# Encoder layer on one core: buffers of the channel mixer as single places in a written order, a chunk's sums moved between products, operands at equal offsets modulo 512 bytes

## The chip, the cores and the metric

One core of a Trainium2 chip runs the whole kernel in one launch. The time is what the device takes for one execution, in microseconds (us). Five engines work side by side, each on its own list of instructions: TensorE (PE; its weight loads are listed as PEld), VectorE (DVE), ScalarE (ACT), GpSimd (POOL) and SyncE (SP). All transfers are issued by SP, one after the other, in the order in which the program writes them.

## The reference, cut to what matters

An encoder layer over 2048 tokens of width 1024: a norm, one input projection, two attention mixers, an output projection with a residual, then the channel mixer.

```python
h = rmsnorm(x, mlp_norm_g[l])
u = jnp.einsum('bsd,df->bsf', h, w_up[l])        # 1024 -> 4096
u = jnp.square(jax.nn.relu(u))
x = x + jnp.einsum('bsf,fd->bsd', u, w_down[l])  # 4096 -> 1024
```

The kernel computes each of the mixer's two products by a scheme with seven block products in place of eight (Strassen's, in Winograd's form): blocks of the left and right operand are first added and subtracted, and the seven results are added up to the four result blocks.

## The kernel before

**Stages.** Input projection (0 to 475 us of the profiled span), attention (to 1812), output projection (1830 to 2044), up projection (2044 to 2696), down projection (to 3352). Every operand of TensorE is split into two parts, high and low (`split`, L151: ScalarE makes a rounded copy, VectorE the remainder), and three matmuls (high by high, high by low, low by high) stand for one.

**Buffers.** `pool(name, n)` reserves n equal buffers; pools on the left side lie one behind the other in the order in which they are made, those on the right side are counted from the other end. A later pool lies over memory that an earlier, closed one left, and the first use of a buffer waits for the last use of what lay there. A tile taken from a pool with several buffers gets one that a planner picks.

**Output projection** (L590). Eight chunks `tc_` of 256 tokens, two blocks of 128 each. `prepare` (L651) loads and splits a chunk's left operand, even chunks into `om_a`, odd ones into `om_b`. `block` (L680) makes 48 matmuls (L691), adds the residual (L695), norms the block on ScalarE (`h_f`, L703, L705), transposes it on TensorE (L171) and stores it as blocks of the right operand (`hb_d`, L716). In the blocks where `th` is 1 (the second 512 tokens of each chunk of 1024, `c` being 0 or 1) it then loads the block's partner (`h_old`) and lets GpSimd make the four sums T1 to T4 (`right_sums`, L757), each stored to `ht_d`. Three products of the up projection are written into the last block (`mlp_first`, L861).

**Up projection** (L865). From here the order of all work is as written. The right operand (tokens) comes in two chunks `c` of 1024 tokens, the left one (weights) in 16 pairs of column groups. There are 16 rounds, rounds 0 to 7 for the first chunk, 8 to 15 for the second; a round has 14 products (r = 0 to 13), of two groups in turn, with 12 matmuls each (L846). In products 0 to 5 the moving operand is one of B11, B21, T2, which lie in `self.first` (pool `uf`, left side); in 6 to 13 it is T3, T1, B22 or T4 in `self.big` (`uh`, right side). The weights' split pieces lie in `uw` and `uw2` (right side). `after(s)` (L907) takes a product's result out of its bank: products i = 0, 2 and 3 of a group are copied by ScalarE (`uy`, L915) and a later product adds to the same bank, which starts it only when the copy is done; 1, 4 and 5 are added on VectorE (L888), all are squared on ScalarE (`act`, L892, L893), and GpSimd makes the sums of the down projection's operand (`us`, L904), stored to `us_d` a few products later. GpSimd also makes the sums of the weights (`up_sums`, L801, at r = 0, 5 and 8). All values of `after` lie in the 15 buffers of `uv`.

**Down projection** (L1059). 56 steps m: seven right blocks i by eight token blocks b, 48 matmuls each (L1147). A step's part of the program: the residual's load (`x1`), the operand's load two steps ahead (`u_load`, into `uf`), in the first 16 steps three loads and two GpSimd operations for a piece of the weights' block T2 (`t2`, L1114; its store is issued after the step's matmuls, and SP waits there for GpSimd), then the loads of the next block's weight pieces (`prepare_piece`, L1004, into `dra` and `drb`), the splits, the matmuls.

Of the kernel before, what the change touches and what calls it, by code (L numbers as in the profile page):

```python
# [46 lines left out]


class Builder:
    def __init__(self, nc, tc, ap):  # L50
        self.nc, self.tc, self.ap = nc, tc, ap

        self.raw, self.ops, self.W, self.PS, self.B, self.U, self.D, self.pending = ({} for _ in range(8))
        self.slots = 0

# [297 lines left out]
    def attention(self):  # L353


        with ExitStack() as es:
# [233 lines left out]
    def out_proj(self):  # L590
# [3 lines left out]
        with ExitStack() as es:  # L594
            pool = self.pools(es)

            m2b, xp, hp, hsp, stage = pool("om_b", 1), pool("ox", 2), pool("oh", 1), pool("ohs", 3), pool("ows", 1)
            wp = [pool(f"ow{j}", 1) for j in range(ND)]
            small = pool("osx", 2)
            psy, pst = pool("psy", 2, space=PSUM), pool("psto", 3, space=PSUM)  # L600

            early = ExitStack()
            pool = self.pools(early)
            mp, sm, m2a = pool("om", 6), pool("osm", 2), pool("om_a", 1)
            pss, psr = pool("psss", 1, space=PSUM), pool("psr", 2, space=PSUM)
# [74 lines left out]
            def block(tc_, b, before=None):  # L680
# [91 lines left out]
    def operand(self, c, n, both=True):  # L772

        if n in self.RIGHT[:3]:
            t = self.first.tile([P, 2, 4, 512], F32R, name=f"hop_{n}", tag="big")
        else:
            t = self.big.tile([P, 2, 4, 512], F32R, name=f"hop_{n}", tag="big")
        src = (self.hb_d if n[0] == "B" else self.ht_d)[c, self.PLACE[n]]
# [16 lines left out]
    def up_load(self, n):  # L795
        if n < 2 * self.NF:
            self.raw[n] = self.raws.tile([P, ND, 256], F32, name="wu_raw", tag="raw")
            f = n % self.NF
            self.dma(self.raw[n], self.ap["w_up"][0, :, f * 256 : f * 256 + 256].rearrange("(j p) f -> p j f", p=P))

    def up_sums(self, n, part):  # L801
# [6 lines left out]
        )  # L808
        x, y = (self.sums.tile([P, 4, P], F32, name="w_sum", tag="sum") for _ in range(2))
        if part == 0:  # L810
# [24 lines left out]
    def up_product(self, s):  # L835
# [3 lines left out]
        if start:  # L839
            pool = self.acc[0] if (n % 2, kind) in ((0, "Y"), (0, "X"), (1, "Y")) else self.acc[1]  # L840
            self.PS[n, kind] = pool.tile([P, 512], F32, name="ps" + kind, tag="acc")
        ps = self.PS[n, kind]
# [8 lines left out]
    def mlp_begin(self, early):  # L851

        early.close()
        self.wop = [self.right("uw", 7)]
        self.acc = [self.right("psua", 3, space=PSUM)]
        for s in range(7):
# [8 lines left out]
    def mlp_up(self, es):  # L865
# [17 lines left out]
        def v(name):  # L883
            return vp.tile([P, H], F32, name=name, tag="v")

# [10 lines left out]
        def store(s, n, name, t):  # L896

            c, f = divmod(n, self.NF)
            dst = self.us_d[self.LEFT.index(name), c * 4 : c * 4 + 4, :, f, :].rearrange("b p t -> p b t")
            later(s, lambda: self.dma(dst, t.rearrange("p (b t) -> p b t", t=P)))  # L900

# [5 lines left out]
        def after(s):  # L907
# [8 lines left out]
            elif i == 1:  # L916
                t = add("c11", ps, x.pop(0))
                x["a11"] = act(t, t)
                store(s + 2, n, "A11", t)
            elif i == 4:  # L920
                t = add("c22", ps, x.pop(3))
                x["z"] = add("z", ps, x.pop(2))
                x["a22"] = act(t, t)
                store(s + 2, n, "A22", t)
            elif i == 5:
                a21 = add("c12", ps, x.pop("z"))
                act(a21, a21)
                s1 = sub(a21, x["a22"], ALU.add)
                s3 = sub(x["a11"], a21)
                x["s2"] = sub(s1, x["a11"])  # L930
                for name, t in (("S1", s1), ("S3", s3), ("S2", x["s2"])):
                    store(s + 4, n, name, t)
            else:
                a12 = act(v("c21"), ps)
                store(s + 2, n, "A12", a12)
                store(s + 5, n, "S4", sub(a12, x["s2"]))
                del val[n]

        for s in self.EARLY:
# [9 lines left out]
        for s in range(last + 1):  # L949
# [54 lines left out]
    def prepare_piece(self, i, k):  # L1004

        terms = self.TERMS[self.ORDER[i]]
        a = self.da.tile([P, 512], F32, name="wd_a")
        self.dma(a, self.w_down(terms[0], k)[:, 0])
        if len(terms) > 1:
            b = self.db.tile([P, 512], F32, name="wd_b")  # L1010
            self.dma(b, self.w_down(terms[1], k)[:, 0])
# [3 lines left out]
    def prepare_early(self, k):  # L1015

        t = self.raws.tile([P, 4, 512], F32, name="wd_raw", tag="raw")
        self.dma(t, self.w_down(self.TERMS[self.ORDER[0]][0], k, 4))
# [3 lines left out]
    def fill_piece(self, i, k):  # L1022
        if not self.quad(i, k):
            self.D[i, k] = self.small_slot()
        elif k % 4 == 0:
            t = self.big.tile([P, 2, 4, 512], F32R, name="wd_q", tag="big")
            for q in range(4):
# [6 lines left out]
    def u_load(self, m):  # L1034
        if m < len(self.STEPS):
            i, b = self.STEPS[m]
            t = self.first.tile([P, 2, 4, 512], F32R, name="u_op", tag="big")
            self.U[m] = t.rearrange("p h a (k t) -> p h (a k) t", t=P)
# [20 lines left out]
    def mlp_down(self):  # L1059
# [4 lines left out]
        with ExitStack() as es:  # L1064
            pool = self.pools(es)
            self.da, self.db, keep, xp = pool("dra", 7), pool("drb", 2), pool("dk", 1), pool("dx", 4)
            psd = pool("psd", 4, space=PSUM)
# [15 lines left out]
            def x1(i, b):  # L1083
# [3 lines left out]
                half, dh = goes[n]  # L1087
                t = xp.tile([P, H], F32, name="x1")
                self.dma(t, self.x1_d[rows(half, b), dh * H : dh * H + H])
# [24 lines left out]
            def t2(k):  # L1114

                a, b, c = self.da.tile([P, H], F32, name="wd_a"), *(self.db.tile([P, H], F32, name="wd_b") for _ in range(2))
                self.dma(a, self.w_down("12", k)[:, 0])
# [7 lines left out]
            for m, (i, b) in enumerate(self.STEPS):  # L1125
                x = x1(i, b)
                if m:
                    self.u_load(m + 2)
                if m < 16:
                    behind.append(t2(m))  # L1130
                if i < 6:

                    for k in (6, 7) if b == 6 else (b,) if b < 6 else ():
                        self.prepare_piece(i + 1, k)
                    for k in {5: (8, 9, 10), 6: (11, 12), 7: (13, 14, 15)}.get(b, ()):
                        self.prepare_piece(i + 1, k)
                if m:
                    self.u_split(m + 1)
# [17 lines left out]
    def build(self):  # L1156
        tc = self.tc
        with tc.tile_pool(name="const", bufs=1) as const, tc.tile_pool(name="dram", bufs=1, space=DRAM) as dram:
# [4 lines left out]
            with ExitStack() as keep, ExitStack() as es:  # L1163

                self.first = self.pools(keep)("uf", 3)
                self.right = self.pools(keep, side="right")
                pool = self.pools(es)
                self.raws, self.sums = pool("uraw", 2), pool("usum", 6)
                self.out_proj()
# [47 lines left out]
```

## Time and profile before

| | |
|---|---|
| median of 3 runs | 3363.14 us (3354.39 to 3369.92) |
| the profiled execution | 3357.71 us, its span 3355.9 |
| TensorE busy | 3238.4 us, 96% |
| VectorE, GpSimd, ScalarE busy | 61%, 51%, 47% |
| transfers | 431.38 MB, mean 129 GB/s |

The span is what the profiler saw of the program, from the first instruction to the last. The rest of the time lies around it. Busy shares are means over stages with different limits; a stage is read from its own rows. A matmul's length in a row is longer than the distance to the next one, since matmuls overlap: the pace is read from start to start.

### The profile page before, as it was taken

The page shows a single profiled execution, that of the slowest core. Times are in us where ns is not written, and L with a number is a line of the kernel's source. Part 1 is how long each engine was busy: PE and PEld are TensorE (multiplying, and loading weights), DVE is VectorE, ACT ScalarE, POOL GpSimd, SP SyncE. Part 2 cuts the span into 40 slices and gives each one's busy share as a digit, 9 for nine tenths or more (in the row PEclk, how much of TensorE's full clock was granted, in tenths as well). Part 3 has the DMA queues.
Part 4 walks back from the last instruction along what each step waited for, and adds up shares of the span by engine and source line. Part 5 has one row for each costly group of instructions (what it writes and reads, how often), then busy time and mean ns, then how long its engine had stood idle before and what let it go on. Part 6 is the DMA issues. An engine that isn't in the chain of part 4 may idle for free. (4 is left out here: it accounts for less than half of the span.)

```text
span 3355.9 us, 43068 instructions
## 1 busy us (share of the span) xinstructions
PE 3238.4 (96%) x15584; PEld 2459.6 (73%) x15584; DVE 2043.7 (61%) x3672; ACT 1576.0 (47%) x2352; POOL 1716.8 (51%) x934
## 2 busy tenths in 40 slices
PE   7999989999999999999999998999899999899999
PEld 6888866666666666666656886888788877688887
DVE  6455547877878777777773554555755554444442
ACT  4222226666666666666664333555555532222221
POOL 3344426666676666766666123666566543314231
PEclk9999999999999999999998998999999999999999
DMA  6336291112112211211013676544645556645573
GB/s 197 109 100 212 88 240 32 29 45 81 43 32 62 73 35 29 77 46 29 29 32 121 213 238 210 151 144 138 226 144 164 180 200 236 237 168 186 202 247 116
DMA packets 402452, 431.38 MB, mean 129 GB/s; under 512 B 26912, under 2 KB 336288, under 8 KB 390336
## 3 DMA queue, kind: packets, MB, share of 16 engines
q1 hardware_dynamic: 402240, 428.64, 41.0%
q8 instruction: 122, 2.00, 0.2%
q14 instruction: 90, 0.74, 0.1%
HBM read 286.93 MB, written 150.01 MB: 130 GB/s over the span
## 5 line engine op out<-in xcount | busy, mean ns | idle before, releaser
L550 POOL TENSOR_TENSOR acc<-acc,pta 128x1024 f32<-128x1024 f32 x224 | 536.7, 2396 | 250.4 <-ACT pta L548 245.4
L1147 PE MATMUL pd<-wd_q,u_op 128*128 128x512 f32 x1728 | 416.1, 399 | 10.0 <-ACT wd_q L153 5.6
L426 DVE CUSTOM_DVE_ANT_0 Sm<-ps_s,T 128x512 f32<-128x512 f32 x512 | 338.2, 685 | 124.0 <-PE ps_s L421 121.8
L1147 PEld LDWEIGHTS pd<-wd_q,u_op 128*128 128x128 f32 x1728 | 328.4, 191 | 91.9 <-ACT wd_q L153 6.5
L548 ACT ACTIVATE pta<-ps_a 128x512 f32<-128x512 f32 x512 | 291.5, 594 | 206.4 <-PE ps_a L547 193.3
L446 POOL TENSOR_TENSOR Sm<-Sm 128x2048 f32<-128x2048 f32 x64 | 293.4, 4584 | 139.4 <-ACT Sm L445 139.4
L514 DVE TENSOR_REDUCE mxa<-ps_m 128x1 f32<-128x512 f32 x512 | 330.3, 683 | 55.8 <-PE ps_m L511 54.6
L421 PE MATMUL ps_s<-Kb,Qb 128*128 128x512 f32 x1024 | 305.7, 408 | 2.7 <-DVE mx L426 2.5
L437 ACT ACTIVATE Sm<-Sm,negm 128x2048 f32<-128x2048 f32 x128 | 256.6, 2005 | 88.2 <-DVE negm L435 80.5
L846 PE MATMUL psY<-hop_T,w_op 128*128 128x512 f32 x1152 | 281.0, 398 | 17.2 <-ACT uy L915 12.1
L557 PE MATMUL po_a<-pta,v_a 128*64 128x512 f32 x1024 | 280.4, 622 | 4.6 <-ACT pta L548 4.4
L846 PEld LDWEIGHTS psY<-hop_T,w_op 128*128 128x128 f32 x1152 | 219.6, 191 | 68.8 <-ACT uy L915 14.2
L546 PEld LDWEIGHTS ps_a<-Qa,Ka 128*128 128x128 f32 x512 | 96.3, 189 | 228.8 <-issue 196.6
L153 ACT CAST u_op<-u_op 128x2048 fp32r<-128x2048 f32 x56 | 106.7, 1907 | 309.4 <-DMA u_op<-us_d 309.4
L546 PE MATMUL ps_a<-Qa,Ka 128*128 128x512 f32 x512 | 233.2, 456 | 17.3 <-DVE vt L154 12.6
L1147 PE MATMUL pd<-w_op,u_op 128*128 128x512 f32 x960 | 234.9, 399 | 7.9 <-ACT w_op L153 4.8
L154 DVE TENSOR_TENSOR w_op<-w_sum,w_op 128x512 fp32r<-128x512 f32 x128 | 151.8, 1197 | 137.8 <-ACT w_op L153 137.7
L154 DVE TENSOR_TENSOR tl<-ptb,th 128x512 fp32r<-128x512 f32 x256 | 175.4, 685 | 79.3 <-ACT th L153 79.1
L1147 PEld LDWEIGHTS pd<-w_op,u_op 128*128 128x128 f32 x960 | 182.2, 190 | 53.5 <-ACT w_op L153 6.0
L475 PE MATMUL po_b<-th,Vb 128*128 128x256 f32 x1024 | 209.4, 288 | 9.3 <-ACT th L153 9.0
L421 PEld LDWEIGHTS ps_s<-Kb,Qb 128*128 128x128 f32 x1024 | 179.5, 191 | 47.0 <-DVE mx L426 11.0
L511 PE MATMUL ps_m<-Ka,Qa 128*128 128x512 f32 x512 | 201.2, 433 | 7.0 <-DVE mx L426 2.3
(229 smaller groups left out, 6905.3 us busy)
## 6 DMA issues: line engine op xcount, KB each, us to landing
u_op<-us_d SPq DMA_DIRECT2D x56, 1024.0 KB, 4.9
wu_raw<-in_w_up SPq DMA_DIRECT2D x32, 1024.0 KB, 6.1
us_d<-us SPq DMA_DIRECT2D x128, 256.0 KB, 3.1
us_d<-c SPq DMA_DIRECT2D x96, 256.0 KB, 6.1
wd_a<-in_w_down SPq DMA_DIRECT2D x96, 256.0 KB, 5.9
Qb<-qkT_d SPq DMA_DIRECT2D x128, 128.0 KB, 3.0
wd_b<-in_w_down SPq DMA_DIRECT2D x64, 256.0 KB, 5.5
Qa<-qkT_d SPq DMA_DIRECT2D x48, 256.0 KB, 4.8
```

The lines of the kernel that those rows point to most:

```text
L154: self.nc.vector.tensor_tensor(lo, src, as32(hi), ALU.subtract)
L421: nc.tensor.matmul(ps, Q[:, c, i, qb * P : (qb + 1) * P], K[c][:, ks], start=(i == 0), stop=(i == 1))
L426: nc.vector.tensor_tensor_reduce(out=Sm[:, ks], in0=ps, in1=T[t0][:, o - t0 : o - t0 + 512], scale=1.0, scalar=BIGNEG, op0=ALU.add, op1=AL ...
L437: nc.scalar.activation(Sm, Sm, AF.Exp, bias=negm, accum_out=l)
L446: nc.gpsimd.tensor_tensor(Pm[0], Pm[0], Pm[1], ALU.add)
L514: nc.vector.tensor_reduce(mx[:, kk : kk + 1], ps, AX.X, ALU.max)
L546: nc.tensor.matmul(ps, K[:, ks], Q[:, i, :], start=True, stop=False)
L548: ex = nc.scalar.activation(pt[:, i, :], ps, AF.Exp)
L550: nc.gpsimd.tensor_tensor(acc, prev if kb == 1 else acc, pt, ALU.add)
L557: nc.tensor.matmul(po[i * HD : (i + 1) * HD, :], v_a[:, kb, g * HD : (g + 1) * HD], pt[:, i, :], start=(kb == 0), stop=(kb == NT - 1),)
L846: self.nc.tensor.matmul(ps, w[:, wk, j, :], b[:, h, j, :], skip_group_check=not start, start=(start and j == 0 and k == 0), stop=(j == 3 a ...
L1147: nc.tensor.matmul(ps, u[:, h, k, :], w[:, g, :], start=(k == 0 and q == 0), stop=(k == NK - 1 and q == 2))
```

## The change

Nine kinds of buffers of the channel mixer become a `Ring`: single-buffer pools that are handed out in a written order, either in turn (weights, operands) or, for the 15 values of the up projection, in the order in which they were given back (`free`). Accumulator banks get a pool each. Three pads (384, 192 and 320 bytes a partition) move what is made after them, so that moving operand and weights of the input projection, the output projection and the channel mixer begin at equal offsets modulo 512 bytes. The second chunk's sums T1 to T4 are no longer made in the output projection's last four blocks: in rounds 1 to 4 of the up projection, `late_sums` loads one block's four parts at r = 5, makes the sums at r = 8 and stores them at r = 11. `oh` has two buffers in place of one. In the output projection and in attention some pools are made in another order. In the down projection the loads of the next block's weight pieces stand ahead of those of T2, and blocks without sums load eight pieces in their last step. The matmuls and their order stay as they are.

```diff
+class Ring:
+    def __init__(self, pool, name, n):
+        self.name, self.places, self.order, self.users = name, [], [], {}
+        self.extend(pool, n)
+    def extend(self, pool, n):
+        k = len(self.places)
+        self.places += [pool(f"{self.name}{q}", 1) for q in range(k, k + n)]
+        self.order += range(k, k + n)
+    def take(self, shape, dtype, name, kept=False):
+        q = self.order.pop(0)
+        t = self.places[q].tile(shape, dtype, name=name, tag=self.name)
+        if kept:
+            self.users[id(t)] = [t, q, 1]
+        else:
+            self.order.append(q)
+        return t
+    def hold(self, t):
+        self.users[id(t)][2] += 1
+    def free(self, t):
+        u = self.users[id(t)]
+        u[2] -= 1
+        if not u[2]:
+            del self.users[id(t)]
+            self.order.append(u[1])
...
+        pool.tile([P, 96], F32, name="const_pad")
         self.lns = pool.tile([P, 1], F32, name="lns")
...
+            pool("spad", 1).tile([P, 48], F32, name="s_pad")
             wp = {g: pool("w" + g, 1) for g in GROUPS}
...
-            scores_b = pool("bk", 3), pool("bt", 1), pool("bq", 2), pool("bs", 6), pool("bsm", 4)
+            bs = pool("bs", 6)
+            scores_b = pool("bk", 3), pool("bt", 1), pool("bq", 2), bs, pool("bsm", 4)
...
-            m2b, xp, hp, hsp, stage = pool("om_b", 1), pool("ox", 2), pool("oh", 1), pool("ohs", 3), pool("ows", 1)
-            wp = [pool(f"ow{j}", 1) for j in range(ND)]
+            m2b, xp, hp, stage = pool("om_b", 1), pool("ox", 2), pool("oh", 2), pool("ows", 1)
+            wp = {j: pool(f"ow{j}", 1) for j in reversed(range(ND))}
             small = pool("osx", 2)
+            pool("opad", 1).tile([P, 80], F32, name="o_pad")
...
-            mp, sm, m2a = pool("om", 6), pool("osm", 2), pool("om_a", 1)
+            m2a, mp, sm = pool("om_a", 1), pool("om", 6), pool("osm", 2)
...
-                if th:
+                if th and not c:
...
-                    new = lambda: hsp.tile([P, 4, P], F32, name="h_sum")
+                    new = lambda: self.sums.take([P, 4, P], F32, "h_sum")
...
-        pool = self.wop[0] if self.slots % 9 < 7 else self.wop[1]
-        self.slots += 1
-        return pool.tile([P, 2, 512], F32R, name="w_op", tag="op")
+        return self.wop.take([P, 2, 512], F32R, "w_op")
...
-        vp = pool("uv", 15)
-        self.wop.append(self.right("uw2", 2))
-        self.big = self.right("uh", 4)
-        self.acc.append(pool("psub", 5, space=PSUM))
+        vp = Ring(pool, "uv", 15)
+        self.wop.extend(self.right, 2)
+        self.big = Ring(self.right, "uh", 4)
+        for k in ((1, "X"), (0, "Z"), (0, "V"), (1, "Z"), (1, "V")):
+            self.acc[k] = pool(f"psu{k[1]}{k[0]}", 1, space=PSUM)
...
         def v(name):
-            return vp.tile([P, H], F32, name=name, tag="v")
+            return vp.take([P, H], F32, name, kept=True)
...
+        def late_sums(s, s_):
+            ts = slice(s_ * P, s_ * P + P)
+            b = [vp.take([P, 4, P], F32, "h_old", kept=True) for _ in range(4)]
+            for i, t in enumerate(b):
+                self.dma(t, self.hb_d[1, i, :, :, ts])
+            def f():
+                t = []
+                def new():
+                    t.append(vp.take([P, 4, P], F32, "h_sum", kept=True))
+                    return t[-1]
+                self.right_sums(*b, new, lambda i, t: None)
+                def g():
+                    for i in range(4):
+                        self.dma(self.ht_d[1, i, :, :, ts], t[i])
+                    for x in t:
+                        vp.free(x)
+                later(s + 6, g)
+                for x in b:
+                    vp.free(x)
+            later(s + 3, f)
...
             elif r == 8:
                 self.up_sums(n0 + 3, 0)
+            if r == 5 and 1 <= s // d <= 4:
+                late_sums(s, s // d - 1)
...
+                if i < 6:
+                    for k in (6, 7) if b == 6 else (b,) if b < 6 else ():
+                        self.prepare_piece(i + 1, k)
+                    sums = len(self.TERMS[self.ORDER[i + 1]]) > 1
+                    for k in ({5: (8, 9, 10), 6: (11, 12), 7: (13, 14, 15)} if sums else {7: range(8, 16)}).get(b, ()):
+                        self.prepare_piece(i + 1, k)
                 if m < 16:
                     behind.append(t2(m))
-                if i < 6:
-                    for k in (6, 7) if b == 6 else (b,) if b < 6 else ():
-                        self.prepare_piece(i + 1, k)
-                    for k in {5: (8, 9, 10), 6: (11, 12), 7: (13, 14, 15)}.get(b, ()):
-                        self.prepare_piece(i + 1, k)
```

## Rows read from the trace of the kernel before

**Rows 1.** Stages: one row per stretch; idle is length less PE busy, PEclk the granted clock

```profile
480.00:530.00 50.00, 40.04 (x140) 24.47 (x141) 39.54 (x117) 26.90 (x28) 11.46 (x3) 0.82 0.60 160
...
2044.00:2092.00 48.00, 34.75 (x127) 26.21 (x125) 22.57 (x20) 18.66 (x24) 18.59 (x13) 0.82 0.72 239
...
2696.00:2716.00 20.00, 16.17 (x51) 10.24 (x50) 13.55 (x16) 9.62 (x18) 6.24 (x4) 0.83 0.86 246
...
2800.00:2920.00 120.00, 107.38 (x429) 83.65 (x428) 51.33 (x38) 30.77 (x31) 48.85 (x26) 0.93 0.71 248
```

**Rows 2.** TensorE's timeline, one round of the up projection: start, length of the group

```profile
2657.43 2.95 PE L846 MATMUL psY<-hop_B,w_op 128*128 128x512 f32 x12
...
2668.62 2.96 PE L846 MATMUL psX<-hop_B,w_op 128*128 128x512 f32 x12
...
2676.95 2.88 PE L846 MATMUL psZ<-hop_T,w_op 128*128 128x512 f32 x12
...
2682.39 5.60 PE L846 MATMUL psY<-hop_T,w_op 128*128 128x512 f32 x24
```

**Rows 3.** TensorE's timeline, output projection: an odd chunk, then an even one

```profile
1972.14 0.39 PE L691 MATMUL py<-wo_lo,m_hi 128*128 128x512 f32 x1
...
1976.00 0.39 PE L691 MATMUL py<-wo_hi,m_hi 128*128 128x512 f32 x1
...
2007.25 0.40 PE L691 MATMUL py<-wo_hi,m_lo 128*128 128x512 f32 x1
...
2010.98 0.40 PE L691 MATMUL py<-wo_hi,m_hi 128*128 128x512 f32 x1
```

**Rows 4.** TensorE's timeline, input projection: first and last of 17 matmuls

```profile
440.01 0.39 PE L252 MATMUL pq<-w_loB,hx_hi 128*128 128x512 f32 x1
...
443.67 0.39 PE L252 MATMUL pq<-w_hiB,hx_lo 128*128 128x512 f32 x1
```

**Rows 5.** TensorE's timeline, three steps of the down projection

```profile
3004.49 5.74 PE L1147 MATMUL pd<-w_op,u_op 128*128 128x512 f32 x24
...
3037.95 2.25 PE L1147 MATMUL pd<-w_op,u_op 128*128 128x512 f32 x9
```

**Rows 6.** Timelines of ScalarE, SP and TensorE, from output projection to up projection

```profile
2052.51 1.06 ACT L703 ACTIVATE h_f<-xo 128x1024 f32<-128x1024 f32 x1 [9.36 <-POOL h_sum L764]
...
2059.50 4.52 SPq L58 DMA_DIRECT2D ht_d<-h_sum  x4
...
2066.41 0.80 SPq L58 DMA_DIRECT2D hop_T<-ht_d  x2
...
2067.32 4.98 PE L846 MATMUL psY<-hop_T,w_op 128*128 128x512 f32 x12 [4.52 <-ACT uy L915]
```

**Rows 7.** Timelines of GpSimd, ScalarE and TensorE, products 8 to 13 of round 4

```profile
2252.79 0.59 ACT L915 COPY uy<-psY 128x512 f32<-128x512 f32 x1 [0.80 <-PE psY L846]
...
2254.56 1.73 POOL L811 TENSOR_TENSOR w_sum<-wu_raw 128x512 f32<-128x512 f32 x1
...
2257.62 1.29 POOL L904 TENSOR_TENSOR us<-c,us 128x512 f32<-128x512 f32 x1
...
2258.03 2.88 PE L846 MATMUL psY<-hop_T,w_op 128*128 128x512 f32 x12
```

**Rows 8.** TensorE's timeline in the down projection: a stall and the matmuls after it

```profile
2883.60 6.94 PE L1147 MATMUL pd<-wd_q,u_op 128*128 128x512 f32 x22 [2.28 <-DVE u_op L154]
2890.38 5.76 PE L1147 MATMUL pd<-w_op,u_op 128*128 128x512 f32 x24
```

**Rows 9.** SP's waits in the down projection (total, times, longest), its issues, TensorE's stall

```profile
SPq L58 <- POOL wd_a L1121: 107.6, 14, 9.1
...
2723.83 0.38 SPq L58 DMA_DIRECT2D u_op<-us_d  x1
...
2795.49 0.38 SPq L58 DMA_DIRECT2D u_op<-us_d  x1
...
2806.41 0.79 PE L1147 MATMUL pd<-w_op,u_op 128*128 128x512 f32 x1 [3.13 <-ACT w_op L153]
```

More of the change, by code (lines that the diff above doesn't have):

```diff
@@ L772, in operand @@
     def operand(self, c, n, both=True):
[L774 to L777, printed above, removed]
+        t = (self.first if n in self.RIGHT[:3] else self.big).take([P, 2, 4, 512], F32R, f"hop_{n}")
         src = (self.hb_d if n[0] == "B" else self.ht_d)[c, self.PLACE[n]]
@@ L796, in up_load @@
         if n < 2 * self.NF:
-            self.raw[n] = self.raws.tile([P, ND, 256], F32, name="wu_raw", tag="raw")
+            self.raw[n] = self.raws.take([P, ND, 256], F32, "wu_raw")
             f = n % self.NF
@@ L808, in up_sums @@
         )
-        x, y = (self.sums.tile([P, 4, P], F32, name="w_sum", tag="sum") for _ in range(2))
+        x, y = (self.sums.take([P, 4, P], F32, "w_sum") for _ in range(2))
         if part == 0:
@@ L853, in mlp_begin @@
         early.close()
-        self.wop = [self.right("uw", 7)]
-        self.acc = [self.right("psua", 3, space=PSUM)]
+        self.wop = Ring(self.right, "uw", 7)
+        self.acc = {k: self.right(f"psu{k[1]}{k[0]}", 1, space=PSUM) for k in ((0, "Y"), (0, "X"), (1, "Y"))}
         for s in range(7):
@@ L899, in store @@
             dst = self.us_d[self.LEFT.index(name), c * 4 : c * 4 + 4, :, f, :].rearrange("b p t -> p b t")
-            later(s, lambda: self.dma(dst, t.rearrange("p (b t) -> p b t", t=P)))
+            def f():
+                self.dma(dst, t.rearrange("p (b t) -> p b t", t=P))
+                vp.free(t)
+            later(s, f)
         def sub(a, b, op=ALU.subtract):
@@ L916, in after @@
             elif i == 1:
-                t = add("c11", ps, x.pop(0))
+                t = add("c11", ps, x[0])
+                vp.free(x.pop(0))
                 x["a11"] = act(t, t)
+                vp.hold(t)
                 store(s + 2, n, "A11", t)
             elif i == 4:
-                t = add("c22", ps, x.pop(3))
-                x["z"] = add("z", ps, x.pop(2))
+                t = add("c22", ps, x[3])
+                vp.free(x.pop(3))
+                x["z"] = add("z", ps, x[2])
+                vp.free(x.pop(2))
                 x["a22"] = act(t, t)
+                vp.hold(t)
                 store(s + 2, n, "A22", t)
             elif i == 5:
-                a21 = add("c12", ps, x.pop("z"))
+                a21 = add("c12", ps, x["z"])
+                vp.free(x.pop("z"))
                 act(a21, a21)
@@ L930, in after @@
                 x["s2"] = sub(s1, x["a11"])
+                vp.hold(x["s2"])
+                for t in (a21, x["a11"], x["a22"]):
+                    vp.free(t)
                 for name, t in (("S1", s1), ("S3", s3), ("S2", x["s2"])):
@@ L934, in after, with f @@
                 a12 = act(v("c21"), ps)
+                vp.hold(a12)
                 store(s + 2, n, "A12", a12)
                 store(s + 5, n, "S4", sub(a12, x["s2"]))
+                vp.free(a12)
+                vp.free(x["s2"])
                 del val[n]
+        def late_sums(s, s_):
[3 more added lines that the diff above has]
+                self.dma(t, self.hb_d[1, i, :, :, ts])
+            def f():
+                t = []
[12 more added lines that the diff above has]
+            later(s + 3, f)
         for s in self.EARLY:
@@ L1006, in prepare_piece @@
         terms = self.TERMS[self.ORDER[i]]
-        a = self.da.tile([P, 512], F32, name="wd_a")
+        a = self.da.take([P, 512], F32, "wd_a")
         self.dma(a, self.w_down(terms[0], k)[:, 0])
         if len(terms) > 1:
-            b = self.db.tile([P, 512], F32, name="wd_b")
+            b = self.db.take([P, 512], F32, "wd_b")
             self.dma(b, self.w_down(terms[1], k)[:, 0])
@@ L1015, in prepare_early @@
     def prepare_early(self, k):
-        t = self.raws.tile([P, 4, 512], F32, name="wd_raw", tag="raw")
+        t = self.raws.take([P, 4, 512], F32, "wd_raw")
         self.dma(t, self.w_down(self.TERMS[self.ORDER[0]][0], k, 4))
@@ L1025, in fill_piece @@
         elif k % 4 == 0:
-            t = self.big.tile([P, 2, 4, 512], F32R, name="wd_q", tag="big")
+            t = self.big.take([P, 2, 4, 512], F32R, "wd_q")
             for q in range(4):
@@ L1036, in u_load @@
             i, b = self.STEPS[m]
-            t = self.first.tile([P, 2, 4, 512], F32R, name="u_op", tag="big")
+            t = self.first.take([P, 2, 4, 512], F32R, "u_op")
             self.U[m] = t.rearrange("p h a (k t) -> p h (a k) t", t=P)
@@ L1065, in mlp_down @@
             pool = self.pools(es)
-            self.da, self.db, keep, xp = pool("dra", 7), pool("drb", 2), pool("dk", 1), pool("dx", 4)
+            self.da, self.db, keep, xp = Ring(pool, "dra", 7), Ring(pool, "drb", 2), pool("dk", 1), Ring(pool, "dx", 4)
             psd = pool("psd", 4, space=PSUM)
@@ L1087, in x1 @@
                 half, dh = goes[n]
-                t = xp.tile([P, H], F32, name="x1")
+                t = xp.take([P, H], F32, "x1")
                 self.dma(t, self.x1_d[rows(half, b), dh * H : dh * H + H])
@@ L1114, in t2 @@
             def t2(k):
-                a, b, c = self.da.tile([P, H], F32, name="wd_a"), *(self.db.tile([P, H], F32, name="wd_b") for _ in range(2))
+                a, b, c = self.da.take([P, H], F32, "wd_a"), *(self.db.take([P, H], F32, "wd_b") for _ in range(2))
                 self.dma(a, self.w_down("12", k)[:, 0])
@@ L1163, in build @@
             with ExitStack() as keep, ExitStack() as es:
-                self.first = self.pools(keep)("uf", 3)
+                self.first = Ring(self.pools(keep), "uf", 3)
                 self.right = self.pools(keep, side="right")
                 pool = self.pools(es)
-                self.raws, self.sums = pool("uraw", 2), pool("usum", 6)
+                self.raws, self.sums = Ring(pool, "uraw", 2), Ring(pool, "usum", 6)
                 self.out_proj()
```

8 lines of the change are left out of this document (3 added, 5 removed).

## The prediction, made before the changed kernel ran

> **What bounds the kernel now.** I read the stage table first (busy time and granted clock per stretch), then TensorE's own timeline, then, where TensorE stands still, the timelines of the engine it waits for. In the steady parts TensorE is never idle, so the kernel loses time in two ways only. One is the pace of a matmul. The other is the seams, where TensorE waits and then runs at half clock: from the end of the output projection into the channel mixer it is busy 34.75 of 48 us at a clock of 0.82, between the projections and attention 40.04 of 50, in the first step of the down projection 16.17 of 20, in its first third 107.38 of 120 [rows 1]. The change touches both and adds two new waits.
>
> **Part 1: alignment.** In one round of the up projection, four products of 12 matmuls whose moving operand lies in `uf` take 11.19 us, 2.80 each, and two whose operand lies in `uh` take 5.44, 2.72 each [rows 2]. Shape, lines and weights' places are the same. What differs can be counted from the buffers' sizes: `uf` begins 96 bytes past a multiple of 512 and the weights of both (`uw`) 480 past one; `uh` lies at 480 too. The output projection says the same: in an even chunk (`om_a` at 416, weights at 96) 16 matmuls take 3.73 us, 233 ns each; in an odd one (`om_b` at 96, weights at 96) 17 take 3.86, 227 ns [rows 3]. The input projection (448 against 128) stands between: 16 in 3.66, 229 ns [rows 4]. The down projection (`uf` at 96, weights at 480) needs 33.46 us for 144, 232 ns [rows 5]. The pads put `uf` at 480, `om_a` and its weights at 480, and the input projection's two operands at 0. If equal offsets give 227 ns:
> up: 16 rounds of 6 products, 0.08 each: 7.7;
> output projection: 384 matmuls of the even chunks, 6 ns: 2.3;
> input projection: 16 blocks of 72 matmuls of this shape, 2.1 ns: 2.4;
> down: 24 matmuls save 0.14, a step of 48 0.27. Only where TensorE sets the pace, steps 18 to 55: 38 steps, 10.4.
> Sum −22.8. The bounds are 0 (the offset is not the cause) and −28 (steps 0 to 17 gain too). I take −23. Attention lies at 96 on both sides already: nothing.
>
> The Trainium skill, page "SBUF — State Buffer", section "SBUF: two separate sides", speaks against this part: inside the engine side only the port pair shared by VectorE and GpSimd makes an engine wait, and TensorE never waits on anyone. It knows no rule by the offset of two operands. By it part 1 saves nothing, which is the third rival below. The trace does not agree: 2.80 against 2.72 at a full clock and without idle time [rows 2].
>
> **Part 2: into the channel mixer.** The 48 us hold 13.3 us of idle time and, with a mean clock of 0.82, about 8.6 of lost clock [rows 1]. The chain: the last block's `h_f` (L703) begins 9.36 us late because `oh` has one buffer and ScalarE waits for the sums of the block before; its store follows, then four stores of sums keep the SP queue for 4.52 us, and only at 2066.41 are the operands T3 and on loaded; TensorE has meanwhile stood 4.52 us for a copy `uy` that sits behind VectorE, which waits for a sum's store [rows 6]. The change gives `oh` two buffers and takes the second chunk's sums out of this stretch: 16 vector operations on GpSimd, 16 stores and 8 loads go from the four last blocks. I work the new order out from the same durations: the last block's transposes come at once, the T3 load is issued about 2055.7, 10.7 us earlier, and I estimate 5 us to its landing and 4 for its split by ScalarE and VectorE; TensorE still waits for it some 2 us, and for the next splits. That ends the seam 11 to 17 us earlier, less half-clock time that any rest of the waits keeps. Bounds −4 (only the wait for `uy` goes) and −18; I take −11.
>
> **Part 3: the second chunk's sums, now in rounds 1 to 4.** Per round: four loads of `h_old` at product 5, four GpSimd operations at product 8, four stores at product 11. GpSimd and the queue have room in total; the question is the order. After product 8 GpSimd makes three operations of `us`, then two of `w_sum` from 2254.56, and reaches the next thing at 2257.62 [rows 7]. There the sums now stand, in front of it: 1.29 each at best. The 15 places are handed out in one written order. Following it through rounds 1 to 4, the copy `uy` after product 10 gets, each time, the place of the second `h_old`, which the third sum reads last. So this copy, now begun at 2252.79, waits until 2257.62 + 3 × 1.29 = 2261.5 and ends at 2262.1. TensorE's product 13 adds to the same bank as that copied one and began at 2258.03 [rows 7]: it stands 4.1 us, with operations of 1.73, as the first of `w_sum` takes, 5.4. Behind the copy ScalarE holds a cast and the next two products' activations. A stall of 2.28 us in the down projection was followed by 22 matmuls in 6.78 us where 5.11 are normal: 1.7 lost to half clock [rows 8]. So each round costs 4.1 + 1.7 = 5.8, four rounds 23. Bounds: 0, if the copy is not held, and 33 with 5.4 and 2.9 of lost clock a round, my estimate for a longer half-clock time. I take +23, since every number of it has its row.
>
> **Part 4: the other buffers of the channel mixer.** At the second chunk's start the order of the work is the same and the stall comes from ScalarE and VectorE: 0. In the first step of the down projection 3.8 us are idle and the clock is 0.83 [rows 1]; a GpSimd operation there waits for a place whose store is still under way, which a written order avoids: −3 (0 to −6).
>
> **Part 5: the loads of the down projection's weights.** SP issues in order, and at the end of each of the first 16 steps it waits for GpSimd's second operation of the T2 weights: 14 times, 107.6 us together. Its cycle is therefore 11.94 us (2723.83 to 2795.49, six steps) against TensorE's 11.15 [rows 9, 5]; it falls back until step 8 stalls 3.13 us on a weight's split [rows 9]. The stretch 2800 to 2920 loses 12.6 us of idle time and, at a clock of 0.93, some 8 of clock to this and to later waits for the same queue [rows 1]. The change puts the step's weight loads ahead of the T2 loads: one issue of 0.4 us and its traffic in front of GpSimd's operations, so a cycle of about 12.5. In the last step of a block without sums, eight loads stand there, and the fifth takes a place that a split of the same step must leave first, so that this cycle takes some 18 instead of 12.5 (steps 7 and 15). From step 1 to 18 I get up to 14 more than before; against it stands that the weights' pieces come earlier, and with them step 8's stall of 3.13 and its half clock may go, 7. Bounds −7 and +25; I take +8.
>
> **Part 6: starts and ends.** `bs` ahead of the other pools of the scores lays their first loads over weights of the input projection that are read to the end; the 10 us lost there [rows 1] become +2 (0 to +12). The output projection's buffers lie over ones free early: −3 (−10 to +8).
>
> **Sum.** −23 −11 +23 −3 +8 −1 = −7. The profiled run took 3357.7 (span 3355.9 and 1.8 around it), so 3350.7; I say 3350. The median of the three runs is 5.4 higher and the runs lie 15 apart; I leave the sum on the profiled run's scale. What a measurement of this kernel can tell from no change is 0.5%, 17 us.
>
> **Rivals.**
> First, faster: GpSimd's sums don't hold ScalarE, because GpSimd comes to them earlier than now or the store and read of a place lie further apart than I follow. For it: GpSimd is idle for almost half of the time. Against: the written order. Then part 3 is 0 and the sum −30: 3328, with part 5 at its ends 3313 to 3345.
> Second, slower: ScalarE, held for 9 us at product 10 in each of four rounds, doesn't catch up before the next round's first copy. What has queued up is 9 us of casts, activations and copies, as long as the time to that copy. TensorE then waits a second time, 4 to 5 us and a second half-clock time. A round costs 12.5, four of them 50, 27 more than in the forecast: 3377, and 3394 with part 5 at +25. The other parts give −30 together, so that it is slower than before from 7.5 us a round on. Against it: ScalarE is busy for half of the time in these rounds.
> Third, no gain from the offsets (the pace has another cause, or the pads put the operands elsewhere): part 1 is 0 and the sum is +16: 3374. Against it are four places of the trace that agree.
>
> **Chances.** Forecast 0.43 (its own range 3335 to 3367), first rival 0.28, second 0.17, third 0.12. Faster by over 0.5%, below 3341: nearly all of the first rival and 0.3 of the forecast, 0.40. Slower, above 3374: three quarters of the second, half of the third, little of the forecast, 0.20. Within: 0.40. The range 3314 to 3378 leaves out the low end of the first rival and the worse half of the second.
>
> **What would show it.** Part 1: 2.72 for each product of a round, 10.9 for a step of the down projection. Part 2: no wait of `h_f` for a sum, and the first full round from about 2080. Part 3: in rounds 1 to 4, and in no other, a wait of the copy `uy` for GpSimd's `h_sum`, a stall ahead of product 13 and a half-clock row. Part 5: the SP queue's wait for GpSimd's T2 operation and the stalls of steps 4 to 17. The prediction is wrong if rounds 1 to 4 run as long as round 6, or if products in `uf` still take 2.80.

## The result, and the profile after

The changed kernel takes 3385.24 us (median of 5 runs, 3381.27 to 3394.82) against 3363.14 before. The ratio, of fast runs alone (in e2 one run of 8809 us is left out), is 1.0077, 95% interval 1.0061 to 1.0092. The changed kernel is slower, outside the range of 3314 to 3378. The profiled execution took 3385.24, with a span of 3383.5 against 3355.9. The 27.6 us lie as follows (lengths read from the starts of TensorE's first and last matmuls of a stage):

| stretch | before | after | difference | forecast |
|---|---|---|---|---|
| to the first score matmul | 488.9 | 495.4 | +6.5 | −0.4 (input projection −2.4, start +2) |
| attention, first score to last matmul | 1322.1 | 1320.0 | −2.1 | 0 |
| from there to the first output matmul | 19.6 | 23.2 | +3.6 | −3 |
| output projection | 213.5 | 216.8 | +3.3 | −2.3 |
| up, round 0 | 62.1 | 50.1 | −12.0 | −11.5 |
| up, rounds 1 to 4 | 154.6 | 176.5 | +21.9 | +21 |
| up, rounds 5 to 15 | 435.3 | 430.8 | −4.5 | −5.3 |
| down, step 0 | 19.6 | 20.1 | +0.5 | −3 |
| down, steps 1 to 17 | 210.8 | 226.5 | +15.7 | +8 |
| down, steps 18 to 55 | 425.3 | 419.9 | −5.4 | −10.4 |

The stage table of the changed kernel (columns as in [rows 1]: length, PE, PEld, DVE, ACT and POOL busy, granted clock, DMA share, GB/s) has, in this order, the seam into attention, round 0, rounds 1 to 4, and the three parts of the down projection:

```profile
480.00:530.00 50.00, 32.65 (x105) 20.22 (x106) 31.20 (x92) 18.87 (x19) 9.11 (x2) 0.69 0.88 211
...
2055.40:2105.50 50.10, 43.68 (x178) 34.38 (x177) 33.28 (x29) 26.95 (x38) 22.17 (x13) 0.93 0.57 179
2105.50:2282.00 176.50, 162.60 (x674) 132.41 (x673) 82.22 (x89) 82.14 (x145) 115.16 (x80) 0.93 0.63 176
2712.80:2732.90 20.10, 15.66 (x50) 9.67 (x49) 13.95 (x16) 9.43 (x17) 6.43 (x5) 0.83 0.84 242
2732.90:2959.30 226.40, 202.15 (x817) 159.99 (x816) 81.16 (x58) 54.91 (x58) 80.19 (x40) 0.94 0.60 211
2959.30:3383.00 423.70, 416.44 (x1825) 342.89 (x1824) 179.57 (x149) 108.19 (x101) 116.68 (x72) 1.00 0.54 188
```

Rounds 1 to 4 were almost without idle time before (154.7 us busy of 154.8); now they hold 13.9 us of it and a clock of 0.93. Timelines of TensorE, GpSimd and ScalarE in round 4 of the changed kernel show why, beside [rows 2, 7]:

```profile
2240.40 2.88 PE L876 MATMUL psX<-hop_B,w_op 128*128 128x512 f32 x12
2243.12 2.88 PE L876 MATMUL psY<-hop_T,w_op 128*128 128x512 f32 x12
...
2274.74 1.26 POOL L800 TENSOR_TENSOR h_sum<-h_old 128x512 f32<-128x512 f32 x1
...
2276.04 0.59 ACT L951 COPY uy<-psY 128x512 f32<-128x512 f32 x1 [5.10 <-POOL h_sum L800]
...
2276.67 5.49 PE L876 MATMUL psY<-hop_T,w_op 128*128 128x512 f32 x12 [3.47 <-ACT uy L951]
```

A product whose operand lies in `uf` takes 2.72 (2240.40 to 2243.12). The copy of product 10 starts the moment the third sum ends, and product 13 starts 0.6 later. It then runs for 5.3 us where 2.7 are normal; the granted clock of that stretch is 0.50, the lower of the two levels. Rounds 1 to 3 show the same stall of 3.47 us.

The two early seams: SP's and TensorE's timelines, first of the kernel before (which [rows 1] show only by their sums), then of the changed one.

```profile
453.34 0.38 SPq L58 DMA_DIRECT2D T<-bias_rep  x1
...
1730.24 21.11 SPq L58 DMA_DIRECT2D wo_raw<-in_w_out  x3
```

```profile
474.72 0.41 SPq L89 DMA_DIRECT2D T<-bias_rep  x1
...
495.43 11.46 PE L456 MATMUL ps_s<-Kb,Qb 128*128 128x512 f32 x32 [18.86 <-DMA Qb<-qkT_d]
...
1777.05 0.37 SPq L89 DMA_DIRECT2D wo_raw<-in_w_out  x1
1806.44 0.33 SPq L89 DMA_DIRECT2D wo_raw<-in_w_out  x1
...
1845.03 0.33 SPq L89 DMA_DIRECT2D wo_raw<-in_w_out  x1
```

The first loads of the scores now go out after the input projection's last matmul (473.5), 21 us later than before, and TensorE stands 18.86 us for them. Of the eight loads of `w_out` three had gone out by 1751; now the second goes out at 1806, and the last at 1845, when the output projection has been running for 6 us.

The SP queue in the down projection, one cycle of it: the kernel before, then the changed one with the queue's waits ahead (to be read beside [rows 9]).

```profile
2747.46 0.37 SPq L58 DMA_DIRECT2D u_op<-us_d  x1
...
2754.27 1.29 POOL L1120 TENSOR_TENSOR wd_a<-wd_a,wd_b 128x512 f32<-128x512 f32 x1 [7.27 <-DMA wd_b<-in_w_down]
2755.64 3.22 POOL L1121 TENSOR_TENSOR wd_a<-wd_b,wd_a 128x512 f32<-128x512 f32 x1
```

```profile
SPq L89 <- POOL wd_a L1199: 147.5, 16, 10.3
...
2753.42 0.42 SPq L89 DMA_DIRECT2D u_op<-us_d  x1
2760.98 3.25 POOL L1198 TENSOR_TENSOR wd_a<-wd_a,wd_b 128x512 f32<-128x512 f32 x1 [7.96 <-DMA wd_b<-in_w_down]
2764.30 1.62 POOL L1199 TENSOR_TENSOR wd_a<-wd_b,wd_a 128x512 f32<-128x512 f32 x1
2766.67 0.33 SPq L89 DMA_DIRECT2D u_op<-us_d  x1
...
2789.99 6.89 PE L1226 MATMUL pd<-w_op,u_op 128*128 128x512 f32 x22 [1.59 <-DVE u_op L187]
...
2815.36 5.30 PE L1226 MATMUL pd<-wd_q,u_op 128*128 128x512 f32 x22 [1.59 <-DVE u_op L187]
...
2825.39 8.80 PE L1226 MATMUL pd<-w_op,u_op 128*128 128x512 f32 x24 [4.73 <-ACT w_op L186]
```

From an operand's load to GpSimd's first operation it is 7.56 us in place of 6.81, the two operations take 4.94 in place of 4.59, and the next operand's load goes out 13.25 after the one before (11.86). Over the same six loads as in [rows 9] the mean cycle is 12.92 in place of 11.94. Step 8 stalls 4.73 in place of 3.13.

### The profile page after: what moved, and what is told of

It is laid out like the page before. It is cut to its first block, busy times and chain, and to the rows that moved or that the text cites. A ratio compares the mean times of both kernels' runs of the same rounds, so it can differ in the third digit from the quotient of the medians.

```text
span 3383.5 us, 43057 instructions
## 1 busy us (share of the span) xinstructions
PE 3235.7 (96%) x15584; PEld 2465.7 (73%) x15584; DVE 2034.7 (60%) x3672; ACT 1578.3 (47%) x2352; POOL 1715.8 (51%) x934
## 5 line engine op out<-in xcount | busy, mean ns | idle before, releaser
L456 PE MATMUL ps_s<-Kb,Qb 128*128 128x512 f32 x1024 | 305.9, 409 | 19.9 <-DMA Qb<-qkT_d 18.9
L1226 PE MATMUL pd<-w_op,u_op 128*128 128x512 f32 x960 | 234.3, 400 | 11.6 <-ACT w_op L186 6.7
L187 DVE TENSOR_TENSOR w_op<-w_sum,w_op 128x512 fp32r<-128x512 f32 x128 | 142.7, 1125 | 129.3 <-ACT w_op L186 129.3
L510 PEld LDWEIGHTS po_b<-th,Vb 128*128 128x128 f32 x1024 | 171.1, 190 | 52.4 <-ACT th L186 26.1
## 6 DMA issues: line engine op xcount, KB each, us to landing
Qb<-qkT_d SPq DMA_DIRECT2D x128, 128.0 KB, 3.0
```

Of the source, the lines that this page charges most:

```text
L187: self.nc.vector.tensor_tensor(lo, src, as32(hi), ALU.subtract)
L456: nc.tensor.matmul(ps, Q[:, c, i, qb * P : (qb + 1) * P], K[c][:, ks], start=(i == 0), stop=(i == 1))
L510: nc.tensor.matmul(po, V[a][:, kb, :], b[:, kk, :], start=(kb == 0 and n == 0), stop=(kb == NT - 1 and n == 2),)
L1226: nc.tensor.matmul(ps, u[:, h, k, :], w[:, g, :], start=(k == 0 and q == 0), stop=(k == NK - 1 and q == 2))
```

## The experiments

The names e1 to e10 stand for runs; each changes the changed kernel only as its diff says, and "rounds" are those of the up projection. Ratios are to the kernel before, on the same chip. e6 to e9 were executed once each, so only their stages are compared. How far a stage varies can be seen from steps 1 to 17 of the down projection: in the six kernels with the same code there (after, e1, e2, e8, e9, e10) they took 225.0 to 229.2.

**e1: sums in place, still at product 8.** The four sums overwrite the loaded parts.

```diff
-                self.right_sums(*b, new, lambda i, t: None)
+                g.tensor_tensor(b11, b12, b11, ALU.subtract)
+                g.tensor_tensor(b12, b22, b12, ALU.subtract)
+                g.tensor_tensor(b22, b22, b11, ALU.subtract)
+                g.tensor_tensor(b21, b21, b22, ALU.subtract)
...
+                later(s + 8, put)
+                later(s + 11, release)
```

> The second chunk's sums stay at product 8 of rounds 1 to 4, but are written over the four loaded parts, which are stored at product 13 and given back two products into the next round; no place read by these sums is handed on within the round. Theory (the copy uy waits for a place that a sum still reads): rounds 1 to 4 fall from 43.4, 44.4, 44.4, 44.4 us to 38.1 to 39 each, total 22 to 24 us less, about 3361. Rival (GpSimd's 5.5 us in front of its next work are what holds TensorE): they stay at 43 to 44 and the time stays.

Rounds 1 to 5: 38.56, 43.27, 43.47, 41.85, 43.48; ratio 1.0076 (1.0061 to 1.0091). The stall at product 13 is gone and stands at product 2 of the next round instead. Timelines of GpSimd, ScalarE and TensorE:

```profile
2196.68 1.25 POOL L940 TENSOR_TENSOR us<-us,c 128x512 f32<-128x512 f32 x1
...
2197.97 0.58 ACT L951 COPY uy<-psY 128x512 f32<-128x512 f32 x1 [5.62 <-POOL us L940]
...
2198.61 4.60 PE L876 MATMUL psY<-hop_T,w_op 128*128 128x512 f32 x12 [3.48 <-ACT uy L951]
```

Neither theory holds as it was put. The named place was the cause of the named stall, but with GpSimd late by its four operations the next place that GpSimd reads, that of `a11`, takes over. Rounds 1 to 5 then lose 20.2 us against five rounds of 38.08, where the changed kernel loses 24.3. So it is the lateness of GpSimd at the moment at which places come round.

**e10: the sums earlier.** As e1, but loaded at product 2, summed at product 5 behind `up_sums`, where GpSimd then stood idle for 4.35 us until the next `us`, stored at 8, given back at 11.

```diff
-            if r == 5 and 1 <= s // d <= 4:
+            if r == 2 and 1 <= s // d <= 4:
...
+                later(s + 6, put)
+                later(s + 9, release)
```

> Only the second chunk's sums changed: parts loaded at product 2, summed in place at product 5, stored at 8, given back at 11. Theory (the price is GpSimd being late when places come round, not the number of its operations): rounds 1 to 4 at 38.1 to 38.6, 22 to 24 us less than the changed kernel, ratio to before about 1.001. Rival: above 41 each.

Rounds 1 to 4: 38.08, 38.08, 38.41, 38.35. Ratio 1.0024 (1.0014 to 1.0033). GpSimd's timeline of e10 in round 3, the first of the four sums and the `us` behind them:

```profile
2212.98 1.29 POOL L997 TENSOR_TENSOR h_old<-h_old 128x512 f32<-128x512 f32 x1
...
2219.10 2.99 POOL L940 TENSOR_TENSOR us<-c,c 128x512 f32<-128x512 f32 x2
```

The same operations and transfers cost 0.6 us there in four rounds, and the profile shows no wait of TensorE in them, which rules out the rival. The ratio fell by some 18 us and not by the 23.6 of these rounds; attention, whose code is the same, took 5.8 us more in e10's profiled execution than in that of the changed kernel.

**e2, e8, e9: orders of pools.** e2 restores both orders, e8 only that of `bs`, e9 only that of `ow`.

```diff
-            bs = pool("bs", 6)
-            scores_b = pool("bk", 3), pool("bt", 1), pool("bq", 2), bs, pool("bsm", 4)
+            scores_b = pool("bk", 3), pool("bt", 1), pool("bq", 2), pool("bs", 6), pool("bsm", 4)
...
-            wp = {j: pool(f"ow{j}", 1) for j in reversed(range(ND))}
+            wp = [pool(f"ow{j}", 1) for j in range(ND)]
```

> bs again behind the other pools of the scores, and ow0 to ow7 again in rising order; all else as changed. Theory (these orders make both early seams longer): first score matmul from 495.4 back to about 489, from the last attention matmul to the first of the output projection 23.1 back to 19.6 us and its first chunk 37.2 back to 34.5; total 11 to 14 less, about 3373. Rival (the second seam is longer because the sums' buffers went, or by the pad): only the first seam comes back, 5 to 8 less.

> Only bs again behind the other pools of the scores; ow0 to ow7 stay in falling order. Theory (bs decides the first seam, by the loads that wait for the input projection's weights): first score matmul at 490 in place of 496. For the second seam, first way (the place of the one staging buffer of w_out decides, over bs in the changed kernel, over bk here): the loads of w_out start at 1735 again and the seam is short, last attention matmul to first output matmul 18 to 20. Second way (the order of ow decides): it stays at 23 or more.

> Only ow0 to ow7 again in rising order; bs stays ahead. Theory: first score matmul stays at 495 to 496. Second seam, first way (staging buffer over bs decides): w_out's second load stays at 1800 or later, seam 23 or more, first chunk 37. Second way (order of ow): 18 to 20 and 34.

| | before | after | e2 | e8 | e9 |
|---|---|---|---|---|---|
| input projection's end to first score matmul | 15.5 | 21.9 | 16.2 | 15.9 | 22.4 |
| last attention matmul to first output matmul | 19.6 | 23.2 | 17.4 | 21.4 | 22.8 |
| first chunk of the output projection | 34.5 | 37.2 | 33.3 | 36.7 | 37.8 |

`w_out`'s first two loads, SP's timeline of e8, then of e9:

```profile
1735.25 0.34 SPq L89 DMA_DIRECT2D wo_raw<-in_w_out  x1
1800.82 0.33 SPq L89 DMA_DIRECT2D wo_raw<-in_w_out  x1
```

```profile
1781.18 0.37 SPq L89 DMA_DIRECT2D wo_raw<-in_w_out  x1
1810.57 0.33 SPq L89 DMA_DIRECT2D wo_raw<-in_w_out  x1
```

`bs` alone decides the first seam. For the second neither of my two ways was right: with `bs` back, the staging buffer is free at 1735, but the split of its row has to go to `ow0`, which lies over a buffer in use until the scores' values end; with `ow` back, the staging buffer itself lies over `bs`. Only both together bring the seam back. e2 as a whole came out at 1.0057 (1.0041 to 1.0073), less gain than the 15 us of its seams: its attention took 1331 us where the other runs took 1320 to 1326, part of it ScalarE standing 2.6 us for a load of `w_out` in the last heads.

**e3, e6: the loads of the down projection.** e3 puts T2's loads first again and spreads pieces 8 to 15 over three steps; e6 only spreads them, so that it has the middle part of this cut alone.

```diff
+                if m < 16:
+                    behind.append(t2(m))
                 if i < 6:
...
-                    for k in ({5: (8, 9, 10), 6: (11, 12), 7: (13, 14, 15)} if sums else {7: range(8, 16)}).get(b, ()):
+                    for k in {5: (8, 9, 10), 6: (11, 12), 7: (13, 14, 15)}.get(b, ()):
...
-                if m < 16:
-                    behind.append(t2(m))
```

> In the down projection the T2 loads again ahead of the next block's weight pieces, and pieces 8 to 15 again spread over the last three steps; all else as changed. Theory (the order of SP's queue sets the pace of steps 1 to 17): from step 1 to step 18 226.5 falls to 207 to 211 us, about 3368. Rival (the steps stall because the faster matmuls run ahead of a queue that is as slow as it was, or because places go in turn): 222 to 226.

> Only the weight pieces 8 to 15 of blocks without sums spread again over the last three steps, with their loads still ahead of those of T2. Theory (the order costs 1.4 us in each cycle of SP, the eight loads 4 to 6 in steps 7 and 15): cycles of steps 7 and 15 fall from 16.4 and 19.7 to 13 to 14, the others stay at 13.3, steps 1 to 17 at 216 to 220. Rival (the eight loads are the whole cost): 210.

Steps 1 to 17: 217.7 in e3, 236.3 in e6, against 226.5 after and 210.8 before. e3's ratio is 1.0041 (1.0026 to 1.0056), and SP's cycles in its steps 1 to 5 are 11.6 to 12.5 long (after: 12.3 to 13.4). e3 thus lies between the theory (207 to 211) and the rival (222 to 226). e3 and e6 differ by the order of the loads alone, which is worth 18.6 us with the pieces spread. With that order the eight loads in one step are no cost against spreading them, they help: spread, four loads of weight pieces stand in front of T2's own three in step 6, and the fourth waits there until its place is free (SP's timeline of e6; the fifth of the row is T2's first), which makes that cycle 19.0 us long. My theory was wrong on this half. e3 still needs 6.9 us more than before in these steps; no run took that apart.

```profile
2809.16 0.38 SPq L89 DMA_DIRECT2D u_op<-us_d  x1
2809.63 11.51 SPq L89 DMA_DIRECT2D wd_a<-in_w_down  x5
```

**e4, e7: the pads.** e4 takes all three out; e7 makes the first 256 bytes, so that `uf` lies at 352 and `uw`, `uh` at 480.

```diff
-        pool.tile([P, 96], F32, name="const_pad")
+        pool.tile([P, 64], F32, name="const_pad")
```

> The three pads taken out, all else as changed. Theory (equal offsets modulo 512 give the pace): rounds 5 to 7 and 10 to 14 of the up projection go from 38.08 back to 38.57, steps of the down projection that do not stall from 10.88 back to 11.15, 128x512 matmuls of the input projection from 228.0 to 229.1 ns; total 14 to 19 more, about 3402. Rival (the single places made it faster): the paces stay and so does the time.

> const_pad 256 bytes in place of 384: uf lies at 352, uw and uh at 480 modulo 512; the operands of the other stages stay equal. Theory (any unequal offset costs): products 0 to 5 of a round 2.80 again, rounds 5 to 7 38.57, steps of the down projection 11.15. Rival (only the offset of before, 96 against 480, was bad): 38.08 and 10.88. Rival (the cost grows with the distance): in between.

e4: 38.57 a round, 11.15 a step, 229.6 ns in the input projection (mean distance of starts, 228.6 with pads); ratio 1.0114 (1.0099 to 1.0129), against 1.0077 with pads. e7: 38.57 and 11.15 to 11.20 too. TensorE's timeline of e7, products 0 and 1, then 8 and 9 of round 8:

```profile
2399.45 2.96 PE L876 MATMUL psY<-hop_B,w_op 128*128 128x512 f32 x12
2402.24 2.97 PE L876 MATMUL psX<-hop_B,w_op 128*128 128x512 f32 x12
...
2428.13 2.88 PE L876 MATMUL psZ<-hop_T,w_op 128*128 128x512 f32 x12
2430.85 2.88 PE L876 MATMUL psV<-hop_B,w_op 128*128 128x512 f32 x12
```

2.79 against 2.72 again. In the channel mixer this other offset is no better than that of before. But not every unequal pair costs as much. In the input projection (448 against 128) it is 229.6 ns against 228.6 with equal offsets. In e4's even chunks `om_a` lies at 288, counted from the buffers' sizes, and the weights at 96: 229.6 ns on the mean, against 233.3 before (416 and 96) and 228.7 with pads. So equal offsets were the fastest in each stage that was compared. The two cheap pairs have one distance in common: the offset of the moving operand (128x512), less that of the other, is 320 modulo 512 in both, and 128, 192 or 384 in the dear ones. No run varied this distance by itself.

**e5: all of it.** e10's sums, e2's orders, e6's spread, and T2's store issued one step later, so that SP comes to it when GpSimd has long been done.

```diff
                 if m < 16:
-                    behind.append(t2(m))
+                store_t2 = [t2(m)] if m < 16 else []
...
-                behind = finish(i, b, ps, x)
+                behind = finish(i, b, ps, x) + store_t2
```

> Five edits on the changed kernel: the second chunk's parts are loaded at product 2, summed in place at product 5, where GpSimd stood idle, stored at 8 and given back at 11; bs and ow0 to ow7 in the order of before; weight pieces 8 to 15 spread over the last three steps; the T2 store is issued one step later, behind the next step's loads, so that SP no longer waits there for GpSimd. Theory: rounds 1 to 4 at 38.1 each (no place is handed on while GpSimd is behind), first score matmul at 490, steps 1 to 17 of the down projection 185 to 200 in place of 226, total about 3326. Rival for the down projection (not SP's wait but the splits and landings set the pace): 215 or more, total 3340 to 3350. Rival for the sums (any four more operations on GpSimd cost TensorE): rounds 1 to 4 stay above 41.

3322.67 us, ratio 0.9879 (0.9862 to 0.9895): faster than both. Stages and SP's waits of e5 (rounds 1 to 4 with 10 us of round 0 and 4 us of round 5; steps 1 to 17):

```profile
2084.80:2252.30 167.50, 167.27 (x734) 137.29 (x733) 90.32 (x97) 90.16 (x159) 124.87 (x87) 1.00 0.70 198
2699.50:2891.00 191.50, 187.68 (x817) 153.96 (x816) 72.33 (x59) 56.70 (x60) 65.09 (x40) 0.99 0.73 255
```

```profile
SPq L89 <- PE pd L1223: 102.0, 16, 9.5
...
SPq L89 <- POOL wd_a L1198: 15.5, 7, 3.7
```

SP's waits are now mostly for TensorE (102.0 us) and little for GpSimd (15.5). Rounds 1 to 4 take 38.4 to 38.6, steps 1 to 17 191.6, and 13 of SP's 16 cycles 10.9 or less. e6 and e5 differ in this stage by the store alone: 236.3 to 191.6. So SP's wait for GpSimd was the main price of these steps, and not the splits or landings. That the same store would free the kernel before is likely from [rows 9], but was not run.

## Why the prediction was wrong

The sum of −7 became +27.6. Four terms failed.

**Part 6, starts and ends: −1 forecast, +12.7 measured** (6.4 at the first seam, 3.6 and 2.6 at the second). This is the step that gives the most. I took the second seam's buffers to lie over ones that are free early, from the order of the pools alone. e8 and e9 show what had to be asked: for the one staging buffer and for the first target of its split, when the last reader of the memory below is done. One of the two being late is enough, since the eight loads pass through that buffer one after the other. For the first seam the reason was right (loads over weights read to the end) and the size was not: a wait of 18.9 us took the place of one of 12.6, and the profile's row of it ends on the loads.

**Part 5: +8 forecast, +15.7 measured.** The direction and the mechanism were right, the cycle was mis-sized: 12.5 forecast, 12.92 on the mean of the first six and 13.4 to 14.0 in steps 8 to 14. I counted the issue of one more load, 0.4. In the cycle shown GpSimd's first operation starts 0.75 later, the two take 0.35 longer together, and the next load goes out 0.29 later behind them. The cycles of steps 7 and 15, 18 forecast, took 16.4 and 19.7; against the alternative of spreading the loads they cost nothing (e6). The stall of step 8, which I hoped might go, grew. And the pace of TensorE, 0.27 a step faster, bought nothing in these steps: without pads they take 227.0 (e4), with pads 226.5.

**Part 1: −23 forecast, about −18 measured.** For the channel mixer the dependence on the offsets is shown (e4, e7): 0.49 a round (0.48 forecast) and 0.27 a step. What failed is the two projections before it: their matmuls went to 228.6 and 228.7 ns on the mean from 229.6 and, in even chunks, 233.3, not to 227. None of it reached the end of the input projection, whose last matmul starts at 473.5 against 473.4; the cause stays open. In the output projection chunks 2 and 6 are 0.42 shorter each, but chunks 4 and 5 have new waits (0.3 for ScalarE's `h_f`, 0.2 for VectorE's `xo`), and chunks 2 to 6 together take 128.0 against 128.2. In e5, without these waits, they take 127.1. In the down projection 5 us more were lost to stalls in steps 18, 48 and 49, which I had not looked at. Of the rule of the Trainium skill in "SBUF — State Buffer", "SBUF: two separate sides", that TensorE never waits on another, the runs show that it does not cover this: the pace changes with the offset of TensorE's own two operands.

**Part 4: −3 forecast, +0.5 measured.** GpSimd's wait for the store is gone, but the operand that it needs next came no sooner. GpSimd's timeline ahead of step 0, the kernel before, then the changed one:

```profile
2688.26 2.55 POOL L904 TENSOR_TENSOR us<-c,c 128x512 f32<-128x512 f32 x2 [21.20 <-DMA us_d<-c]
```

```profile
2705.41 2.55 POOL L940 TENSOR_TENSOR us<-c,c 128x512 f32<-128x512 f32 x2 [21.17 <-ACT c L924]
```

Its wait is as long, now for ScalarE's `c`, and the operation ends about as near to the first matmul of the step as it did (4.8 us ahead of it, 5.2 before).

**Right:** part 2 (`h_f` no longer waits for a sum; round 0 −12.0, less 0.9 for transposes that now lie in the output projection) and part 3, by mechanism and place: 43.4, 44.4, 44.4 and 44.4 against 38.08 without it are 24.2, forecast 23. That the size came so near is in part luck. In rounds 2 to 4 TensorE stood 3.6 us where I had 4.1, and lost 2.6 to the half clock where I had 1.7; the two misses nearly cancel. e1 corrects one more thing: the place that I named is one of two that would have stalled.

The second rival's time came near, but not by its mechanism: ScalarE caught up in each round, with no second stall. The first and third rival did not occur.

What stays open: e5 still loses 8 us in steps 48 and 49 (14.2 and 15.7 against 10.9), and the input projection's end does not move with its faster matmuls.

## What to carry to other kernels

Where buffers are handed out in one written order, look for each take at which engine reads that place last and how late that engine is at that moment; here the same work cost 0.6 us at the engine's idle time and 24 in front of a place's last read. A store in an in-order queue that waits for an engine holds every load behind it: issue it a step later, behind those loads (here 236.3 us against 191.6). When pools change their order, follow what lies under the first buffers of the next stage, above all under a single staging buffer and the first target after it.

## What was not expected of the hardware

In the up and down projection a 128x512 matmul takes 226.7 ns from start to start where moving operand and weights begin at the same offset modulo 512 bytes, and 232 to 233.5 where one lies at 480 and the other at 96 or at 352: 2 to 3% more, in a stream without idle time at full clock. Two other unequal pairs cost less, as said at e7: 229.6 against 228.6 and 228.7. After a stall of 3.47 us, the next 12 matmuls took 5.3 us, 2.6 of them lost to the half clock, in rounds 2 to 4 alike; after the same stall in round 1 it was 4.4 and 1.7. Stalls of 1.59 in the down projection were followed by it in some steps and not in others: in the fence on the SP queue above, the 22 matmuls after one took 6.89, after another of the same length 5.30.
